# A new address layout for the gate block of a decoder layer, with two raw weight tiles instead of three

## The chip, the cores and the metric

The kernel runs on one NeuronCore of one Trainium2 chip. The metric is the device time of one execution in microseconds (us). A profiled execution also gives the span, from the first to the last recorded instruction, and the granted clock of TensorE as a share of full speed.

The engines are named as in the profile: PE is the matrix engine (PEld its weight loads), DVE the vector engine, ACT the scalar engine, POOL GpSimd. SP issues most of the DMAs. Each engine, and each engine's DMA issues, run strictly in the order in which the program was written out.

## The reference

One layer over 1024 tokens of width 1024, in 32-bit floats. After an RMSNorm giving `h`, three branches (a chunked mLSTM, a differential attention, a cross-attention into memory) are computed, merged by gates, and followed by an MLP:

```python
h = rms_norm(x, norm_mix_g[l])
...
g_m, g_d, g_c = jnp.split(jax.nn.sigmoid(h @ w_gate[l] + b_gate[l]), N_BRANCH, axis=-1)
merged = g_m * (y_m @ w_proj_m[l]) + g_d * (y_d @ w_proj_d[l]) + g_c * (y_c @ w_proj_c[l])
x = x + merged @ w_out[l]
h2 = rms_norm(x, norm_mlp_g[l])
x = x + jnp.square(jax.nn.relu(h2 @ w_up[l])) @ w_down[l]
```

The gates `sigmoid(h @ w_gate + b_gate)` have 3 x 1024 columns. The last 1024 columns (the gate `g_c`) are what the block around this change computes.

## The kernel before

Every float matrix product is made of three matmuls: each operand is split into a rounded part and a remainder, `hi` (a cast on ACT) and `lo` (a subtraction on DVE), and `mm3` adds hi*hi, hi*lo and lo*hi in PSUM. So every weight and every activation passes through one ACT cast and one DVE subtraction before PE reads it (`split`, lines 113 and 114).

The stages follow one another on PE: input norms and memory keys, branch C, branch M, branch D (the attention, with matmuls of the gates and of the next head woven between), then the **gate block** (`wino_gates`, line 1142), then the **tail** (`tail`, line 1405): the three branch projections in the order C, M, D, the output projection, and the MLP.

The gate block uses a Winograd form of the 2 x 2 block product: four units `u`, each with seven products `j` (12 matmuls of 128x512 each) in the order of `PROD`. Its tiles, per SBUF partition:

- `X[4]`, `X[5]`, `X[6]`, `X[3]`: sums of blocks of `h`, 16,384 bytes each, loaded from DRAM (`hc_d`) and split in place. A unit's products 0, 1 and 6 read `hT` itself, product 2 reads X[4], 3 reads X[5], 4 reads X[6] and 5 reads X[3].
- `fr`: raw weights, 8,192 bytes each. Eight of them are loaded (two DMAs each), numbered 2u+kk; POOL adds four derived blocks (lines 1161 to 1164). A ring of three is used. `load(n+3)` is issued when the last of the seven blocks of raw n has been split.
- `w`: the split weights, in a ring of 13 tiles shared with the stages before; 14 are made per unit by `wsp`, and they run ahead of PE by as much as the ring allows.
- `ev`: four evaluation tiles `u2`, `c11`, `u3`, `c21` of 2,048 bytes, with two buffers each. Each product's PSUM bank is added into one of them by DVE (the first by an ACT copy). PE alternates between two PSUM banks, so a product can begin only when the product two before it has been added.
- `gt`: two tiles of 2,048 bytes for the tanh of a finished output, which ACT stores to DRAM (`gates`), on its own DMA queue.

**Addresses set the order of loads.** A pool takes the next free bytes upward. A tile placed on bytes that an earlier, closed pool has used must wait for those users. With `reuse_waits="tile"` (branch D's and the gate block's pools) a tile waits only for the users of earlier tiles on its own bytes. Without it (all the tail's pools) **every** tile of the new pool waits for **every** user of every closed pool that the new pool touches.

`hT` fills 3,072 to 68,608, the ring of 13 `w` tiles 68,608 to 108,544, the ring of raw weights up to 117,760. Above it first lie branch D's pools, and then, over them, the gate block's: in the kernel before `gt` (117,760), `ev` (121,856), X[3] (138,240), X[6] (154,624), X[5] (171,008), X[4] (187,392), `fr` 0 to 2 (203,776 to 228,352).

The tail then lays its own pools over everything: nine single tiles `ys` for a branch's split rows (`kt`, 8,192 bytes each, from 96,768 to 170,496, filled from the top one down), `yrp` with two raw row tiles `kraw` (170,496 to 178,688), `rp2` with two raw weight tiles `raw` (178,688 to 186,880), `wp2` with four split weight tiles `w` (186,880 to 219,648). For each branch `k_tiles` (line 1377) loads eight row tiles of 512 KB through `kraw` and splits them into `kt`; `load_w` (line 132) loads the weights; `group` runs the matmuls, the first group with k outermost, so that PE can start with one `kt` and one `w`.

Only PE's order is pinned by hand in the gate block. The orders of ACT, DVE, POOL and of the DMA issues are set by the framework's planner, which places each instruction by its own estimate of when its inputs are there.

Of the kernel before, what the change touches and what calls it, by code (L numbers as in the profile page):

```python
# [10 lines left out]
F32 = mybir.dt.float32  # L11
# [6 lines left out]
P = 128  # L18
# [13 lines left out]
def f32(ap):  # L32
    return ap.bitcast(F32)
# [40 lines left out]
class Layer:  # L74
# [487 lines left out]
    def m_gates2(self, pool):  # L562
# [5 lines left out]
        self.nc.vector.tensor_copy(self.gcol, ps2[:, 0 : 3 * W])  # L568

    def branch_m(self, pool, gp, tail, gnext):  # L570
        nc, a = self.nc, self.a
        V, G = nc.vector, nc.gpsimd
# [569 lines left out]
    def wino_gates(self, base):  # L1142

        nc, V, A, G = self.nc, self.nc.vector, self.nc.scalar, self.nc.gpsimd
        one = lambda name, bufs=1: base.enter_context(tc.tile_pool(name=name, bufs=bufs, reuse_waits="tile"))
        tc = self.tc
        gtp, ev, x3, x6 = one("fgt", 2), one("fev", 2), one("fx3"), one("fx6")
        x5, x4, r0, r1, r2 = one("fx5"), one("fx4"), one("fr0"), one("fr1"), one("fr2")
        rr = Ring([r2, r1, r0])
        X = {}  # L1150
        for q, p in ((4, x4), (5, x5), (6, x6), (3, x3)):
            X[q] = p.tile([P, 4, 2, 512], F32R, tag="x", name=self.name("hx"))
        raws, W = {}, []

        def load(n):
            if n < 8:
                u, kk = divmod(n, 2)
                r = rr.tile([P, 8, 2, P], F32, tag="fr", name=self.name("fr"))
                for i in range(2):
                    nc.sync.dma_start(r[:, 0:4, i], self.a["wgq"][u][:, 2 * kk + i])  # L1160
                G.tensor_add(r[:, 4], r[:, 0], r[:, 3])
                G.tensor_sub(r[:, 5], r[:, 4], r[:, 1])
                G.tensor_sub(r[:, 6], r[:, 1], r[:, 0])
                G.tensor_sub(r[:, 7], r[:, 2], r[:, 5])
                raws[n] = r

        def wsp():
            n = len(W)
            if n < 56:
                u, r = divmod(n, 14)  # L1170
                j, kk = divmod(r, 2)
                t = self.wp.tile([P, 2, 256], F32R, tag="w", name=self.name("w"))
                self.split(t[:, 0], t[:, 1], raws[2 * u + kk][:, 1 + self.PROD[j][0]].rearrange("p k n -> p (k n)"))
                W.append(t)
                if j == 6:
                    load(2 * u + 3 + kk)

        def x_(q, kp, i):
            if q >= 3:
                return X[q][:, kp, i]  # L1180
            k, hf = divmod(q + 1, 2)
            return self.hT[:, 2 * kp + k, i, hf * 512 : hf * 512 + 512]

        for n in range(3):
            load(n)
        for q in (4, 5, 6, 3):
            k, h = ((0, 1), (1, 0), (0, 0), (1, 1))[q - 3]
            r = f32(X[q][:, :, 1])
            nc.sync.dma_start(r, self.hcd[:, k, :, h * 512 : h * 512 + 512].rearrange("k p n -> p k n"))
            for i in (0, 2):  # L1190
                self.split(X[q][:, i : i + 2, 0], X[q][:, i : i + 2, 1], r[:, i : i + 2])
        for _ in range(9):
            wsp()
        self.pinned = True
        tl = lambda n: ev.tile([P, 512], F32, tag=n, name=self.name(n))
        for u in range(4):
            def out(i, c):
                ft, s = 16 + u * 2 + i // 2, slice(i % 2 * 512, i % 2 * 512 + 512)
                t = gtp.tile([P, 512], F32, tag="gt", name=self.name("gt"))
                A.activation(t, c, AF.Tanh, bias=self.bg[:, ft : ft + 1], scale=0.5)  # L1200
                nc.scalar.dma_start(self.gdr[ft, :, s], t)

            for j, (l, q) in enumerate(self.PROD):
                ps = self.mm_tile()
                for kp in range(4):
                    w = W[u * 14 + 2 * j + kp // 2]
                    c = slice(kp % 2 * P, kp % 2 * P + P)
                    self.mm3(ps, (w[:, 0, c], w[:, 1, c]), (x_(q, kp, 0), x_(q, kp, 1)), kp == 0, kp == 3)
                    if kp % 2:
                        wsp()  # L1210
                if j == 0:
                    u2, c11, u3, c21 = (tl(n) for n in ("u2", "c11", "u3", "c21"))
                    A.copy(u2, ps)
                elif j == 1:
                    V.tensor_add(c11, u2, ps)
                    out(1, c11)
                elif j == 2:
                    V.tensor_add(u2, u2, ps)
                elif j == 3:
                    V.tensor_add(u3, u2, ps)  # L1220
                elif j == 4:
                    V.tensor_add(c21, u3, ps)
                    out(3, c21)
                elif j == 5:
                    V.tensor_add(u3, u3, ps)
                    V.tensor_add(u2, u2, ps)
                    out(2, u3)
                else:
                    V.tensor_add(u2, u2, ps)
                    out(0, u2)  # L1230
        self.pinned = False
# [180 lines left out]
    def tail(self):  # L1412
        tc, nc, a = self.tc, self.nc, self.a
# [10 lines left out]
        with ExitStack() as c0:  # L1424
            E = lambda *x, **k: c0.enter_context(tc.tile_pool(*x, **k))
            one = E(name="tone", bufs=1)
# [7 lines left out]
            with ExitStack() as c1:  # L1434
                E = lambda *x, **k: c1.enter_context(tc.tile_pool(*x, **k))
                self.pmm, self.kmm, self.nmm = Banks(E, "pmm2"), 8, 3
                if True:
# [4 lines left out]
                    hole = E(name="hole", bufs=1).tile([P, 7 * 256], F32, name="hole")  # L1442
                    V.memset(hole[:, 0:1], 0.0)
                    ysp = Ring([E(name=f"ys{i}", bufs=1) for i in range(9)][::-1])
                    rawp = E(name="yrp", bufs=2)
                    self.rp = E(name="rp2", bufs=2)
                    self.wp = E(name="wp2", bufs=4)
                    hi = [[mtp.tile([P, 512], F32R, name=f"mh{k}_{hf}") for hf in range(2)] for k in range(NK)]
# [43 lines left out]
            with ExitStack() as c1:  # L1492
                E = lambda *x, **k: c1.enter_context(tc.tile_pool(*x, **k))
# [237 lines left out]
    def run(self):  # L1731
        tc, nc = self.tc, self.nc
        with ExitStack() as ctx:
            E = lambda *x, **k: ctx.enter_context(tc.tile_pool(*x, **k))
# [22 lines left out]
            with ExitStack() as c1:  # L1757
# [37 lines left out]
                with tc.tile_pool(name="wpg", bufs=13, reuse_waits="tile") as self.wp, tc.tile_pool(name="rpg", bufs=3, reuse_waits="tile") as self.rp:  # L1795
                    self.gwp, self.grp = self.wp, self.rp
                    with ExitStack() as c3:
                        E3 = lambda name, bufs: c3.enter_context(tc.tile_pool(name=name, bufs=bufs, reuse_waits="tile"))
                        pdo, pdy, pd, pd3, pdm = E3("pdo", 2), E3("pdy", 1), E3("pd", 2), E3("pd3", 3), E3("pdm", 1)
                        pdv2, pds, pd5, pdv = E3("pdv2", 17), E3("pds", 1), E3("pd5", 7), E3("pdv", 5)  # L1800
                        self.tmask = pdm.tile([P, D], F32, name="tmask")
                        nc.gpsimd.memset(self.tmask, 0.0)
                        nc.gpsimd.affine_select(
                            out=self.tmask[:, D - P : D], in_=self.tmask[:, D - P : D], pattern=[[-1, P]],
                            compare_op=ALU.is_ge, fill=NEG, base=0, channel_multiplier=1,
                        )
                        self.pd4 = None
                        class T4:
                            def tile(_, shape, dt, tag, name):
                                tag = "dscr2" if tag == "gt" else tag  # L1810
                                p = {
                                    "draw": pd5, "drr": pdv, "dv": pdv2, "dk": self.pd4, "dpe1": pdm, "daT": pd3, "dst": pd3,
                                    "dscr": pds, "dsg": pds, "dscr2": pdy, "y": pdy, "doS": pdo, "dso": pdo,
                                }.get(tag, pd)
                                return p.tile(shape, dt, tag=tag, name=name)
                        self.gpool = T4()
                        kv, done = [], [0]
                        gemm = self.d_gemm(self.gpool, kv, done)
                        next(gemm)
                        sums = self.h_sums(self.gpool)  # L1820
                        for n in range(32):
                            next(self.gates)
                            if n % 2 == 0:
                                next(sums)
                        cg.close()
                        self.pd4 = E3("pd4", 4)
                        self.branch_d(T4(), sums, gemm, kv, done)
                    with ExitStack() as c3:
                        self.wino_gates(c3)
# [70 lines left out]
```

## Time and profile before

| | |
|---|---|
| median of 3 runs | 2200.8 us (2197.91 to 2201.39) |
| the profiled execution's own time | 2198.07 us |
| its span | 2196.3 us, 30710 instructions |
| busy share of the span: PE, DVE, ACT, POOL | 98%, 65%, 46%, 26% |
| mean granted clock of TensorE | 0.996 |
| gate block on PE | from about 1127 to 1206 us |
| first projection group of the tail on PE | from about 1207 us |

A row of the timeline shows the start, the duration, the engine, the line of the kernel, the operation, what it writes and reads, and in brackets how long the engine had been idle and what ended that. Rows of equal instructions are merged (x36 is 36 of them). A row of the windows view gives, for a stretch of time, its length, the busy time and instruction count of PE, PEld, DVE, ACT and POOL, the granted clock, the mean busy share of the DMA engines and what they moved in GB/s.

### The profile page before, as it was taken

The page shows a single profiled execution, that of the slowest core. Times are in us where ns is not written, and L with a number is a line of the kernel's source. Part 1 is how long each engine was busy: PE and PEld are TensorE (multiplying, and loading weights), DVE is VectorE, ACT ScalarE, POOL GpSimd, SP SyncE. Part 2 cuts the span into 40 slices and gives each one's busy share as a digit, 9 for nine tenths or more (in the row PEclk, how much of TensorE's full clock was granted, in tenths as well). Part 3 has the DMA queues.
Part 4 walks back from the last instruction along what each step waited for, and adds up shares of the span by engine and source line. Part 5 has one row for each costly group of instructions (what it writes and reads, how often), then busy time and mean ns, then how long its engine had stood idle before and what let it go on. Part 6 is the DMA issues. An engine that isn't in the chain of part 4 may idle for free.

```text
span 2196.3 us, 30710 instructions
## 1 busy us (share of the span) xinstructions
PE 2154.0 (98%) x11049; PEld 1853.4 (84%) x11049; DVE 1424.0 (65%) x2678; ACT 1002.6 (46%) x1998; POOL 571.6 (26%) x732
## 2 busy tenths in 40 slices
PE   7999999999999999999999999999999999999999
PEld 5878889898899999999887788888787888788887
DVE  6643565575548777777665433554589877867779
ACT  6543354454346666666554221223444444643332
POOL 2100000000111111111121002202757655665553
PEclk9999999999999999999999999999999999999999
DMA  6123122121443343333343643435435444954444
GB/s 245 37 72 116 60 89 70 44 82 49 157 119 92 96 97 86 86 87 80 108 158 121 206 144 125 139 115 190 155 116 199 157 144 153 330 192 157 145 140 168
DMA packets 137358, 281.46 MB, mean 128 GB/s; under 512 B 13137, under 2 KB 29814, under 8 KB 135158
## 3 DMA queue, kind: packets, MB, share of 16 engines
q1 hardware_dynamic: 130870, 259.58, 37.5%
q10 hardware_dynamic: 6336, 19.93, 2.3%
q8 instruction: 87, 1.43, 0.3%
q14 instruction: 65, 0.53, 0.1%
HBM read 182.95 MB, written 71.34 MB: 116 GB/s over the span
## 4 chain that ended last, share of the span: by engine, by line
PE 79%; DMA 7%; DVE 6%; ACT 3%; POOL 2%; issue 2%; SPq 0%; DVEq 0%; ACTq 0%; POOLq 0%
PE mm L93 46%; PE p L93 21%; PE sc L93 6%; PE po L93 3%; PE tp L96 3%; DMA x_d<-gl 1%; DVE acc L69 1%; DVE wo L69 1%; DMA gl<-in_xT 1%; PE pr L96 1%; DMA xr<-h_d 1%; DVE u L69 1%; DMA kraw<-y 1%; POOL wraw L1262 0%; DVE w L114 0%
## 5 line engine op out<-in xcount | busy, mean ns | idle before, releaser
L93 PE MATMUL mm<-w,hT 128*128 128x384 f32 (+3 forms) x2496 | 472.9, 332 | 2.9 <-ACT w L113 2.4
L93 PE MATMUL mm<-hT,w 128*128 128x512 f32 x1680 | 411.8, 396 | 0.0
L93 PEld LDWEIGHTS mm<-w,hT 128*128 128x128 f32 x2496 | 390.2, 190 | 14.5 <-ACT w L113 3.0
L93 PEld LDWEIGHTS mm<-hT,w 128*128 128x128 f32 x1680 | 308.5, 188 | 64.7
L93 PE MATMUL p<-xo,wo 128*128 128x512 f32 x1344 | 309.7, 392 | 3.1 <-DVE u L69 1.6
L93 PE MATMUL p<-xd,wo 128*128 128x512 f32 x1344 | 307.8, 391 | 3.8 <-DVE u L69 1.9
L93 PEld LDWEIGHTS p<-xd,wo 128*128 128x128 f32 x1344 | 252.9, 189 | 58.5 <-DVE u L69 2.6
L93 PEld LDWEIGHTS p<-xo,wo 128*128 128x128 f32 x1344 | 252.2, 189 | 59.3 <-DVE u L69 3.7
L93 PE MATMUL mm<-kt,w 128*128 128x512 f32 x1152 | 264.5, 391 | 4.0 <-ACT kt L113 2.7
L93 PEld LDWEIGHTS mm<-kt,w 128*128 128x128 f32 x1152 | 216.8, 189 | 51.7 <-ACT kt L113 3.8
L113 ACT CAST w<-raw 128x256 fp32r<-128x256 f32 (+3 forms) x272 | 142.2, 545 | 164.7 <-PE mm L93 123.2
L114 DVE TENSOR_TENSOR w<-raw,w 128x256 fp32r<-128x256 f32 (+3 forms) x272 | 162.7, 619 | 80.0 <-ACT w L113 78.6
L106 ACT CAST wo<-wraw 128x896 fp32r<-128x896 f32 x122 | 115.0, 944 | 206.6 <-PE p L93 112.0
L69 DVE TENSOR_TENSOR wo<-wraw,wo 128x896 fp32r<-128x896 f32 x122 | 144.3, 1200 | 57.0 <-ACT wo L106 57.0
L1260 POOL TENSOR_TENSOR wraw<-wraw 128x128 f32<-128x128 f32 x128 | 95.1, 743 | 238.4 <-DMA wraw<-in_wdown 103.5
L1008 ACT ACTIVATE dpe<-sc,dst,drr 128x256 f32<-128x256 f32 (+7 forms) x128 | 106.8, 834 | 97.6 <-DVE dst L1004 95.4
L129 POOL TENSOR_SCALAR hss<-hss 128x4 f32<-128x4 f32 x8 | 3.3, 411 | 416.0 <-ACT mscr L754 273.3
L1000 DVE CUSTOM_DVE_ANT_0 sc<-sc,tmask 128x256 f32<-128x256 f32 (+7 forms) x128 | 97.0, 758 | 13.3 <-PE sc L93 12.6
L1263 POOL TENSOR_TENSOR wraw<-wraw 128x128 f32<-128x128 f32 x128 | 93.9, 733 | 10.0
L93 PE MATMUL sc<-dk,dq 128*128 128x512 f32 (+3 forms) x384 | 92.2, 348 | 0.0
L1262 POOL TENSOR_TENSOR wraw<-wraw 128x128 f32<-128x128 f32 x128 | 91.8, 717 | 0.0
L106 ACT CAST xd<-xd 128x1536 fp32r<-128x1536 f32 (+2 forms) x36 | 54.9, 1528 | 67.7 <-DMA xd<-r_d 67.7
(308 smaller groups left out, 3087.6 us busy)
## 6 DMA issues: line engine op xcount, KB each, us to landing
dk<-dsg SPq DMA_DIRECT2D x64, 256.0 KB, 4.5
wraw<-in_wup SPq DMA_DIRECT2D x64, 256.0 KB, 3.3
r_d<-xts SPq DMA_DIRECT2D x16, 1024.0 KB, 4.1
wraw<-in_wdown SPq DMA_DIRECT2D x64, 256.0 KB, 3.0
xd<-r_d SPq DMA_DIRECT2D x19, 768.0 KB, 7.3
xd<-r_d SPq DMA_DIRECT2D x14, 1024.0 KB, 7.0
raw<-in_wd SPq DMA_DIRECT2D x32, 384.0 KB, 3.2
kraw<-y SPq DMA_DIRECT2D x24, 512.0 KB, 4.5
```

What stands on the lines that cost most here:

```text
L69: return self.tc.keep_in_program_order(f(*a, **k))
L93: self.pin(self.nc.tensor.matmul(out, l, r, start=start, stop=stop))
L96: self.pin(self.nc.tensor.transpose(out, x, self.ident))
L106: self.A.copy(hi, src)
L113: nc.scalar.copy(hi, src)
L114: nc.vector.tensor_sub(lo, src, f32(hi))
L129: g.tensor_scalar(r, ss, 1.0 / width, EPS, op0=ALU.mult, op1=ALU.add)
L1000: V.tensor_tensor_reduce(out=sc[:, 0:n], in0=sc[:, 0:n], in1=self.tmask[:, D - n : D], scale=1.0, scalar=-3.0e38, op0=ALU.add, op1=ALU.max ...
L1008: nc.scalar.activation(pe[c][:, 0:n], sc[:, 0:n], AF.Exp, bias=t8[:, 2 + c : 3 + c], scale=rr[:, i, c : c + 1], accum_out=t8[:, 4 + c : 5 ...
L1260: G.tensor_add(r[:, 4], r[:, 0], r[:, 3])
L1262: G.tensor_sub(r[:, 6], r[:, 1], r[:, 0])
L1263: G.tensor_sub(r[:, 7], r[:, 2], r[:, 5])
```

## The change

Three places change, and all of them are allocations.

1. The gate block's pools are opened in another order. From 117,760 upward: one evaluation pool `ev1` (8,192 bytes), a pad of 128 bytes, X[3], X[6], X[4], `r0`, `r1`, X[5], `gt`, and the second evaluation pool `ev0`. The two evaluation buffers are now two pools, used in turn by units 0, 2 (`ev0`) and 1, 3 (`ev1`). The ring of raw weights has two tiles, used in the order r1, r0; a raw is loaded when the raw two before it has been split. The pad gets one memset.
2. In the tail `yrp` holds three raw row tiles instead of two; `rp2` and `wp2` move up by 4,096 bytes.
3. In branch D the pools `pd` (with `dpe0` and `dq`, two buffers each) and `pd3` (with `daT` and `dst`, three buffers each) change places.

```diff
-        gtp, ev, x3, x6 = one("fgt", 2), one("fev", 2), one("fx3"), one("fx6")
-        x5, x4, r0, r1, r2 = one("fx5"), one("fx4"), one("fr0"), one("fr1"), one("fr2")
-        rr = Ring([r2, r1, r0])
+        ev1, pad, x3, x6, x4, r0, r1, x5, gtp, ev0 = (
+            one(f"f{n}", 2 if n == "gt" else 1)
+            for n in ("ev1", "pd", "x3", "x6", "x4", "r0", "r1", "x5", "gt", "ev0")
+        )
+        nc.vector.memset(pad.tile([P, 32], F32, tag="pad", name="fpd")[:, 0:1], 0.0)
+        rr, ev = Ring([r1, r0]), (ev0, ev1)
...
-                    load(2 * u + 3 + kk)
+                    load(2 * u + 2 + kk)
...
-        for n in range(3):
+        for n in range(2):
             load(n)
...
-        tl = lambda n: ev.tile([P, 512], F32, tag=n, name=self.name(n))
         for u in range(4):
+            tl = lambda n: ev[u % 2].tile([P, 512], F32, tag=n, name=self.name(n))
...
-                    rawp = E(name="yrp", bufs=2)
+                    rawp = E(name="yrp", bufs=3)
...
-                        pdo, pdy, pd, pd3, pdm = E3("pdo", 2), E3("pdy", 1), E3("pd", 2), E3("pd3", 3), E3("pdm", 1)
+                        pdo, pdy, pd3, pd, pdm = E3("pdo", 2), E3("pdy", 1), E3("pd3", 3), E3("pd", 2), E3("pdm", 1)
```

## The prediction

> **What bounds the kernel now.** I read the page's first lines, then the windows view by stage, then PE's timeline where the windows show it idle.
>
> ```profile
> span 2196.3 us, 30710 instructions
> ...
> 600.00:1045.00 445.00, 444.53 (x2845) 430.36 (x2844) 335.80 (x980) 270.21 (x687) 67.56 (x61) 1.00 0.38 96
> 1045.00:1127.00 82.00, 80.52 (x417) 67.76 (x416) 54.27 (x113) 45.50 (x92) 13.76 (x17) 1.00 0.42 136
> 1127.00:1206.00 79.00, 78.34 (x345) 63.99 (x343) 41.03 (x76) 33.80 (x70) 17.14 (x21) 1.00 0.34 115
> 1206.00:1234.00 28.00, 24.27 (x93) 18.23 (x94) 12.80 (x13) 11.36 (x12) 0.04 (x1) 0.94 0.69 241
> 1234.00:1500.00 266.00, 266.00 (x1175) 220.23 (x1174) 110.34 (x125) 55.65 (x63) 28.03 (x28) 1.00 0.41 134
> ```
>
> PE sets the time. The change can win only what PE loses between 1045 and 1234 us: 1.5 us idle at the end of branch D, 0.7 in the gate block, 3.7 at the start of the tail. From 1234 to 1500 PE is never idle, and 266.00 us / 1175 = 0.2264 us per matmul is the pitch I use; a product of 12 takes 2.72 us.
>
> ```profile
> 1108.08 1.01 PE L93 MATMUL po<-dv,daT 128*128 128x128 f32 x7 [1.36 <-DVE daT L114]
> 1156.35 8.48 PE L93 MATMUL mm<-hx,w 128*128 128x512 f32 x36 [0.43 <-DVE c L1215]
> 1202.89 2.88 PE L93 MATMUL mm<-hT,w 128*128 128x512 f32 x12
> 1206.78 1.17 PE L93 MATMUL mm<-kt,w 128*128 128x512 f32 x4 [1.00 <-POOL ones L1428]
> 1208.13 5.52 PE L93 MATMUL mm<-kt,w 128*128 128x512 f32 x21 [0.18 <-DVE kt L114]
> 1215.80 16.42 PE L93 MATMUL mm<-kt,w 128*128 128x512 f32 x63 [2.15 <-ACT kt L113]
> 1232.73 7.59 PE L93 MATMUL mm<-kt,w 128*128 128x512 f32 x32 [0.51 <-ACT kt L113]
> ```
>
> The start of the tail loses more than its idle time. From the end of the gate block (1202.89 + 2.88 = 1205.77) to 1240.32 PE runs 4 + 21 + 63 + 32 = 120 matmuls, 27.2 us at the pitch, in 34.55: **7.4 us lost**, of which 3.84 are the bracketed waits. The rest are slow matmuls:
>
> ```profile
> 1213.00:1218.00 5.00, 2.85 (x11) 2.03 (x10) 3.45 (x3) 2.22 (x3) 0.00 (x0) 0.93 1.03 410
> 1218.00:1223.00 5.00, 5.00 (x17) 3.90 (x17) 0.20 (x1) 0.00 (x0) 0.00 (x0) 0.73 0.68 226
> ```
>
> After the gaps the granted clock falls to 0.93 and 0.73; 5 x 0.07 + 5 x 0.27 = 1.7 us go there. The DMA engines are full (share 1.03).
>
> So all that can be won is 1.36 + 0.43 + 7.4 = 9.2 us, 0.4%.
>
> **The change, part by part.** *Start of the tail.* What does each tail pool wait for?
>
> ```profile
> 1197.65 0.82 SPq L139 DMA_DIRECT2D raw<-in_wpc  x2
> 1200.37 0.80 SPq L1383 DMA_DIRECT2D kraw<-y  x2
> 1201.69 1.05 ACT L113 CAST w<-raw 128x1024 fp32r<-128x1024 f32 x1 [7.96 <-DMA raw<-in_wpc]
> ```
>
> Before, `rp2` (178,688 to 186,880) lies on X[5] alone, and the raws are issued 8.12 us before the gate block's end, three products: exactly when X[5] is done. `yrp` touches X[6] by 512 bytes, and the row loads go out two products before the end, when X[6] is done. `wp2` lies on X[5], X[4] and raws, so its casts wait only for data. The rows come too late: that is the 2.15 and the 0.51.
>
> Afterwards `yrp` (170,496 to 182,784) lies on X[4] and r0. X[4] is last read by product 2, so the row loads can go out at 1205.77 - 4 x 2.72 = 1194.9, 5.5 us earlier, and three at once. The first five `kt` tiles lie on X[4], X[6] and X[3] and are free by 1203. `rp2` (182,784 to 190,976) lies on r0 and r1, free after the last weight split. All this moves away from PE's path. But `wp2` (190,976 to 223,744) now lies on r1, X[5], **`gt`** and `ev0`, and its tiles wait for every user of them, the last store of `gt` to DRAM among them. That store closes the chain of the last product:
>
> ```profile
> 1206.25 0.68 DVE L1229 TENSOR_TENSOR u<-u,mm 128x512 f32<-128x512 f32 x1
> ...
> 1207.62 0.72 ACT L1200 ACTIVATE gt<-u,dv 128x512 f32<-128x512 f32 x1 [0.94 <-DMA gates<-gt]
> ...
> 1208.37 0.33 ACTq L1201 DMA_DIRECT2D gates<-gt  x1
> ...
> L1201 ACTq DMA_DIRECT2D gates<-gt x16: 326/326/387, 1136.7 to 1208.4; - x16
> ...
> DMA to landing us min/median/max: 2.0/2.0/6.5
> ```
>
> PE's first tail matmul then comes after the add (0.68), the tanh up to its store's issue (1208.37 - 1207.62 = 0.75), the landing, and the cast of `w` (1.05). The landing has a median of 2.0 and a maximum of 6.5, the high values while the row loads fill the DMA engines; with those out of the way earlier I take 3.0. The gap is 0.68 + 0.75 + 3.0 + 1.05 = 5.5 us. Queued behind the waiting cast on ACT are only later casts, whose rows are there by then, so PE loses nothing after the gap except the clock, 1.7 as in the rows above. 5.5 + 1.7 = 7.2 lost, against 7.4: **-0.2 us**. Ends: landing 2.0 and no clock loss give 4.5, or -2.9; landing 6.5 gives 9.0 + 1.7, or +3.3.
>
> The Trainium skill speaks against this part (DMA: Bandwidth & Descriptors, Anatomy of one DMA): a transfer's semaphore rises only when the last byte is confirmed in memory, slowest for HBM, with about 2.0 us fixed and the bytes at 436 GB/s on top (fitted there for GpSimd's path; ACT issues this one). Worked out from that page, the 256 KB store would be an estimated 2.6 us and this part -0.6; the trace agrees in part only, with a median of 2.0 below the page's figure and a maximum of 6.5 far above.
>
> *Gate block, ring of two.* A raw's DMAs, its POOL sums and the split that waits:
>
> ```profile
> 1154.32 0.71 ACT L113 CAST w<-fr 128x256 fp32r<-128x256 f32 x2 [2.91 <-DMA fr<-in_wgq]
> ...
> 1154.76 0.94 DVE L114 TENSOR_TENSOR w<-fr,w 128x256 fp32r<-128x256 f32 x1 [2.90 <-ACT w L113]
> 1155.63 0.67 DVE L1215 TENSOR_TENSOR c<-u,mm 128x512 f32<-128x512 f32 x1
> ...
> 1158.85 1.30 DVE L114 TENSOR_TENSOR w<-fr,w 128x256 fp32r<-128x256 f32 x2
> 1160.07 0.68 DVE L1220 TENSOR_TENSOR u<-u,mm 128x512 f32<-128x512 f32 x1
> ...
> 1154.68 0.74 POOL L1161 TENSOR_TENSOR fr<-fr 128x256 f32<-128x256 f32 x1 [13.37 <-DMA fr<-in_wgq]
> ...
> 1159.83 0.92 POOL L1162 TENSOR_TENSOR fr<-fr 128x256 f32<-128x256 f32 x1
> ```
>
> Before, at each unit's change one raw was a unit ahead, and only the other was just in time: its load starts when the split of the last block but one ends, lands 2.91 us too late for ACT, and the add of product 1 behind it on DVE costs PE 0.43. The weights themselves have 13 tiles of lead, so PE never misses a weight; it misses the adds queued behind a late split. Afterwards both raws are just in time. The first lands when the just-in-time one lands now, so the 0.43 stays about what it is. The second raw's sums come behind the first's on POOL, as the second pair here: its block for product 2 (L1162) is ready at 1159.83 + 0.92 = 1160.75 instead of about 1157. The cast (0.41, half of 0.71 and a little), the slow subtraction (0.94) and the add of product 3 (L1220), which stands behind that subtraction on DVE, end at 1162.8. PE wants that bank two products after 1156.35 + 2.72, at 1161.8: **1.0 us** lost per change of unit. There are three. The planner may put an add ahead of a split; I take two thirds, **+2.0**, between -0.4 (all adds ahead) and the second rival's +8.2.
>
> *End of branch D.*
>
> ```profile
> 1067.87 27.32 SPq L1160 DMA_DIRECT2D fr<-in_wgq  x6
> 1096.32 0.37 SPq L1189 DMA_DIRECT2D hx<-hc_d  x1
> 1108.67 2.16 SPq L1189 DMA_DIRECT2D hx<-hc_d  x3
> ...
> 1100.35 4.21 DVE L114 TENSOR_TENSOR w<-fr,w 128x256 fp32r<-128x256 f32 x5
> ...
> 1105.08 2.35 DVE L114 TENSOR_TENSOR hx<-hx 128x1024 fp32r<-128x1024 f32 x2
> 1107.35 0.68 DVE L114 TENSOR_TENSOR daT<-tp,daT 128x512 fp32r<-128x512 f32 x1
> ...
> 1117.36 1.05 ACT L113 CAST hx<-hx 128x1024 fp32r<-128x1024 f32 x1 [1.59 <-DMA hx<-hc_d]
> ```
>
> Before, raws 1 and 2 and X[4] lie on branch D's last keys, and the other X on its values, until 1109. Afterwards X[5] lies on the keys and X[6] on `dpe0` (moved up by the exchange of pools), so both load before 1106, while r0 and X[4] lie on value tiles: raw 1, X[4] and X[3] load last. They are wanted at 1128 or later, so nothing starves. The 1.36 us came from five weight splits at 0.84 each and an X split ahead of `daT` on DVE. One raw fewer means fewer splits and no POOL sums there: **-1.0**, between -1.36 and +1.6 (ACT's longest wait for an X, 1.59, landing on PE).
>
> *The rest.* The pad's memset, the third `kraw` in the later branches and the later start of the block sums of `h` under the exchanged pools cost 0: PE is full from 600 to 1045 and from 1234 to 1500, and the sums are read only from 1096. If that cover went, a memset is the least of it. The MLP's pools meet the same users, the last raw and the last weight of the output projection, 4,096 bytes higher.
>
> Sum: -0.2 + 2.0 - 1.0 = **+0.8 us**, on the profiled 2198.07 (span 2196.3 and 1.8 around it). The median lies 2.7 above the profiled execution, so I forecast 2200.8 + 0.8 = **2201.6 us**.
>
> **Rivals.** *The tail wins.* The last store lands in 2.0 us, the clock holds, and the adds stay ahead in the gate block: -2.9 - 0.4 - 1.4 = -4.7, 2196.1. For it: all rows are in SBUF before PE asks. Against: a gap of 4.5 us where gaps of 2.15 already dropped the clock.
>
> *The ring of two stalls PE (the slower side).* Place: DVE's queue at the three changes of unit. If the add of product 1 stands behind the split of the **second** raw, which lands one weight (half a product, 1.36) later, it ends at 1154.76 + 1.36 + 0.94 + 0.67 = 1157.7 instead of 1155.92, PE's need (1156.35 - 0.43): 1.8 us, and with the 1.0 above, 2.8 to 2.9 per change, 8.6 in all, less today's 0.43: +8.2; with the other parts 2207.8. It decides from the point where the add's end passes 1155.92. For it: today's add already stands behind a late split. Against: the planner sees the second load start later and can reorder.
>
> *The layout moves only what is hidden.* If `wp2`'s wait is met early or replaces an equal one, and the adds keep their slack, nothing moves: 2200.8.
>
> **How the numbers follow.** Forecast 0.53, hidden 0.14, ring stalls 0.18, tail wins 0.15. The forecast's own range is 2198 to 2206. About 0.2% (4.4 us) is what a measurement can tell from no change: below 2196.4 is faster, above 2205.2 slower. Faster: most of the tail's win and a little of the forecast, 0.14; slower: 0.15 of the ring's 0.18 and 0.07 of the forecast, 0.22; the same 0.64. The range 2195 to 2208.5 reaches both rivals.
>
> **What would show it.** The first `w` cast of the tail waits for a store of `gt`, and PE has one gap of 4.5 to 6 us at 1206 instead of four small ones, with no wait for `kt` behind it. Row loads leave near 1195. In the gate block PE waits for the adds of lines 1215 and 1220 near 1136, 1156 and 1175 after POOL's second set of sums. The 1.36 us before `po` shrinks. A first tail matmul before 1208, or PE idle over 4 us between 1127 and 1206, would prove the forecast wrong.

## The result, and the profile after

The changed kernel takes 2205.5 us (median of 18 runs, 2202.1 to 2209.8); 18 runs of the kernel before, taken beside them, have a median of 2199.4. The ratio is **1.0025, 95% interval 1.0018 to 1.0032**: 6.1 us slower, where +0.8 was forecast. The profiled execution took 2206.7 us. The page's first line, then the windows view (length, then busy time and count of PE, PEld, DVE, ACT and POOL, clock, DMA share, GB/s):

```profile
span 2204.9 us, 30710 instructions
```

```profile
600.00:1045.00 445.00, 444.34 (x2843) 430.18 (x2842) 334.66 (x979) 270.84 (x688) 67.92 (x61) 1.00 0.38 95
...
1125.00:1207.00 82.00, 80.62 (x344) 63.55 (x342) 43.95 (x78) 34.41 (x71) 19.86 (x25) 1.00 0.42 136
1206.00:1211.00 5.00, 0.69 (x4) 0.23 (x2) 3.32 (x5) 3.67 (x5) 0.20 (x1) 0.84 0.90 291
1211.00:1216.00 5.00, 0.00 (x0) 0.00 (x0) 1.23 (x1) 1.12 (x2) 0.00 (x0) 0.50 1.00 390
1216.00:1221.00 5.00, 4.67 (x13) 3.34 (x14) 4.75 (x5) 4.01 (x5) 0.00 (x0) 0.64 0.48 158
1221.00:1250.00 29.00, 29.00 (x130) 24.01 (x129) 9.17 (x10) 4.21 (x4) 0.00 (x0) 1.00 0.55 182
```

PE is full up to 1045 and again from 1221, as before. Between 1206 and 1216 it does almost nothing: 0.69 us of work in ten, with the DMA engines at 0.90 and 1.00 and the granted clock at 0.84 and 0.50. Timeline of the changed kernel, PE first, then the chain that ends the gap (its lines lie three higher: L1218 and L1223 are L1215 and L1220 of the kernel before):

```profile
1104.69 2.21 PE L93 MATMUL po<-dv,daT 128*128 128x256 f32 x16 [0.20 <-DVE daT L114]
...
1135.22 9.02 PE L93 MATMUL mm<-hx,w 128*128 128x512 f32 x36 [0.43 <-DVE c L1218]
...
1155.37 9.02 PE L93 MATMUL mm<-hx,w 128*128 128x512 f32 x36 [0.15 <-DVE c L1218]
...
1175.54 9.04 PE L93 MATMUL mm<-hx,w 128*128 128x512 f32 x36 [0.16 <-DVE c L1218]
...
1203.80 2.90 PE L93 MATMUL mm<-hT,w 128*128 128x512 f32 x12
1216.31 46.00 PE L93 MATMUL mm<-kt,w 128*128 128x512 f32 x194 [9.62 <-ACT w L113]
...
1195.59 9.83 SPq L1386 DMA_DIRECT2D kraw<-y  x6
...
1206.66 1.23 DVE L114 TENSOR_TENSOR kt<-kraw,kt 128x1024 fp32r<-128x1024 f32 x1 [0.40 <-ACT kt L113]
1207.81 0.68 DVE L1232 TENSOR_TENSOR u<-u,mm 128x512 f32<-128x512 f32 x1
1207.92 4.98 SPq L1386 DMA_DIRECT2D kraw<-y  x3
1208.18 1.04 ACT L113 CAST kt<-kraw 128x1024 fp32r<-128x1024 f32 x1 [0.93 <-DMA kraw<-y]
1209.13 0.72 ACT L1203 ACTIVATE gt<-u,dv 128x512 f32<-128x512 f32 x1
1209.88 0.33 ACTq L1204 DMA_DIRECT2D gates<-gt  x1
1215.17 1.04 ACT L113 CAST w<-raw 128x1024 fp32r<-128x1024 f32 x1 [3.88 <-DMA gates<-gt]
```

Read from the top:

- The wait for `po` at the end of branch D fell from 1.36 to 0.20: 1.2 us won.
- In the gate block each change of unit shows a short wait for an add, and rows of 36 matmuls that take 9.02 us (8.48 before). The block ran from 1124.88 to 1203.80 + 2.90 = 1206.70, 81.8 us against 78.7: **3.1 lost**. Not all of this is waiting, as the rows below show.
- At the start of the tail the first `w` cast waits for the last store of `gt`, and PE for that cast: one gap of 9.62 us. From 1206.70 to 1216.31 + 46.00 = 1262.31 are 55.6 us; 194 matmuls at the pitch of 0.2264 are 43.9. **11.7 lost**, against 7.4 before: 4.3 more.

The last unit of the gate block has no change of unit behind it and waits for nothing in either kernel. Its 48 matmuls on X, before:

```profile
1192.01 11.04 PE L93 MATMUL mm<-hx,w 128*128 128x512 f32 x48
```

and after:

```profile
1192.61 11.35 PE L93 MATMUL mm<-hx,w 128*128 128x512 f32 x48
```

They take 0.31 us longer. Four units of this are 1.2 of the 3.1, in matmuls that read X at its new places; the other 1.9 is waits and what they slow down.

The three bullets make 6.2 us. The two spans differ by 8.6; the rest is in a place that the prediction held to be full. Groups view of PE between 1540 and 1600 us (the step from the output projection to the MLP; the last figures are idle time and what ended it), before:

```profile
L93 PE MATMUL px<-ones,ssq 128*128 128x1 f32 x16 | 2.1, 251 | 2.2 <-POOL ssq L1483 1.7 <-DVE gl L1476 0.5
```

and after:

```profile
L93 PE MATMUL px<-ones,ssq 128*128 128x1 f32 x16 | 2.9, 302 | 5.0 <-DVE gl L1479 3.3 <-POOL ssq L1486 1.7
```

2.8 us more. Whether the change did this is taken up behind the experiments.

### The profile page after: what moved, and what is told of

Read it like the earlier page. It is cut to its first block, busy times and chain, and to the rows that moved or that the text cites. A ratio compares the mean times of both kernels' runs of the same rounds, so it can differ in the third digit from the quotient of the medians.

```text
span 2204.9 us, 30710 instructions
## 1 busy us (share of the span) xinstructions
PE 2153.2 (98%) x11049; PEld 1851.8 (84%) x11049; DVE 1424.0 (65%) x2679; ACT 1001.6 (45%) x1998; POOL 572.5 (26%) x732
## 3 DMA queue, kind: packets, MB, share of 16 engines
q8 instruction: 87, 1.43, 0.3%
## 4 chain that ended last, share of the span: by engine, by line
PE 82%; DMA 7%; DVE 5%; ACT 2%; POOL 2%; issue 2%; SPq 0%; DVEq 0%; POOLq 0%; ACTq 0%
PE mm L93 47%; PE p L93 22%; PE sc L93 6%; PE po L93 3%; PE tp L96 3%; DVE acc L69 1%; DMA gl<-in_xT 1%; DMA xr<-h_d 1%; DMA fr<-in_wgq 1%; DVE wo L69 1%; PE pr L96 1%; DMA x_d<-gl 1%; DVE u L69 1%; DVE w L114 1%; PE tp L93 0%
## 5 line engine op out<-in xcount | busy, mean ns | idle before, releaser
L1263 POOL TENSOR_TENSOR wraw<-wraw 128x128 f32<-128x128 f32 x128 | 91.5, 715 | 232.2 <-DMA wraw<-in_wdown 101.7
L1266 POOL TENSOR_TENSOR wraw<-wraw 128x128 f32<-128x128 f32 x128 | 91.1, 712 | 9.9
L1265 POOL TENSOR_TENSOR wraw<-wraw 128x128 f32<-128x128 f32 x128 | 92.8, 725 | 0.0
L1264 POOL TENSOR_TENSOR wraw<-wraw 128x128 f32<-128x128 f32 x128 | 87.9, 687 | 0.0
```

## The experiments

My theory after the result: most of the loss is the tail's `w` casts, which wait for a store of `gt` because the tail's pools have no waits by tile; the ring of two costs the gate block some 2 to 3 us; the shorter wait for `po` is a gain. Rivals: the ring alone makes the loss; the third row tile makes it (more row loads in flight); the layout merely shifts the order of the plan. The table holds all runs; the readings of single profiles are made as above: the gate block from PE's rows, the tail's loss from the end of the gate block to about 1262 us against 0.2264 us per matmul.

| kernel | median, us | ratio to before, 95% | gate block | lost at start of tail | wait `po` | waits `px` |
|---|---|---|---|---|---|---|
| before | 2199.4 | | 78.7 | 7.4 | 1.36 | 2.2 |
| after | 2205.5 | 1.0025 (1.0018 to 1.0032) | 81.8 | 11.7 | 0.20 | 5.0 |
| e1: waits by tile for `wp2` | 2203.5 | 1.0018 (1.0005 to 1.0032) | 80.9 | 7.8 | 0.27 | 4.1 |
| e2: `gt` lowest | 2194.9 | 0.9976 (0.9963 to 0.9990) | 80.5 | 0.1 | 0.34 | 0.0 |
| e3: third raw weight | 2205.3 | 1.0019 (1.0005 to 1.0033) | 79.3 | 11.5 | 0.24 | 3.8 |
| e4: e2 and e3 | 2192.4 | 0.9966 (0.9954 to 0.9978) | 79.3 | 0.0 | none | 1.1 |
| e5: before, ring of two | 2202.9 | 1.0018 (1.0003 to 1.0032) | 80.2 | 5.3 | 1.36 | 3.6 |
| e6: before, three row tiles | 2198.3 | 0.9994 (0.9983 to 1.0005) | 78.6 | 3.7 | 1.75 | 1.5 |
| e7: before, `pd` and `pd3` exchanged | 2199.2 | 0.9995 (0.9985 to 1.0005) | 78.2 | 4.7 | 1.69 | 0.6 |
| e8: after, two row tiles | 2206.6 | 1.0032 (1.0021 to 1.0043) | 81.7 | 13.4 | none | 3.2 |
| e9: after, `pd` and `pd3` as before | 2208.5 | 1.0042 (1.0027 to 1.0056) | 81.2 | 12.1 | 0.18 | 4.7 |
| e10: e4, two row tiles | 2195.9 | 0.9988 (0.9975 to 1.0001) | 79.2 | 3.2 | 0.17 | 3.6 |

The ratios are against runs of the kernel before in the same batch (medians 2200.6 for e1 to e4, 2199.8 for e5 to e8, 2198.4 for e9 and e10). e1 to e10 have 12 runs each, e9 six.

### e1: the wait for the store taken away

```diff
-                    self.wp = E(name="wp2", bufs=4)
+                    self.wp = E(name="wp2", bufs=4, reuse_waits="tile")
```

> The changed kernel, except that the split weights of the tail wait only for users of their own bytes; addresses and all orders stay. Theory (the first casts wait for the last store of gt): the cast no longer waits 3.9 us at 1211 to 1215, but it still stands behind the row casts on ACT, so PE starts at about 1212.4 instead of 1216.3; about 4 us of the gap of 9.6 go, and the time falls by 3.5 to 5 us, to about 2201. Rival 1 (the ring of two costs it, the gap only shows what comes late anyway): PE waits for rows instead, less than 1 us is won. Rival 2 (the DMA engines are overfull from earlier rows): the gap stays above 8 us.

Timeline of e1:

```profile
1207.21 0.33 ACTq L1204 DMA_DIRECT2D gates<-gt  x1
...
1208.53 1.04 ACT L113 CAST w<-raw 128x1024 fp32r<-128x1024 f32 x1
...
1209.67 1.19 PE L93 MATMUL mm<-kt,w 128*128 128x512 f32 x2 [4.93 <-issue]
```

The cast no longer waits for the store's landing (it ends at 1209.57, and PE starts 0.1 us later, though the bracket names no releaser), and the gap is 4.93 instead of 9.62 us. The tail's loss falls by 3.9, to 7.8, no lower than before's. Every engine keeps the order of the changed kernel here, so the first `w` cast still stands on ACT behind the `kt` casts and the last tanh, and starts when these are done; its raws had left at 1187.72, 20 us earlier, so it was not short of data. So the wait is one part of the trouble, and the **order** that the planner chose for a cast that it believed late is, by this reading, the other; no run changes the order alone. The median fell by 2.0 us only, less than the 3.5 to 5 expected, and the intervals of the two ratios overlap.

### e2: `gt` opened first

```diff
-        ev1, pad, x3, x6, x4, r0, r1, x5, gtp, ev0 = (
+        gtp, ev1, pad, x3, x6, x4, r0, r1, x5, ev0 = (
```

(with the names in the same order). `gt` then lies at 117,760, under the `kt` tiles, and `wp2` no longer touches it.

> The changed kernel with gt opened first, at 117,760, so that the tail's weights no longer lie on it; all else above moves up by 4,096 bytes. Theory: neither the wait for the store nor the late place in ACT's queue is left, the casts follow the end of X[5] as before the change, and the rows come early; the gap falls from 9.6 to under 1.5 us, the clock holds, and 9 to 10.5 us are won, to about 2196. Rival 1: under 1 us won. Rival 2: rows still late, a gap of 3 to 5 us with waits for kt, 4 us won at most.

Timeline of e2:

```profile
1197.71 2.01 ACT L113 CAST w<-raw 128x1024 fp32r<-128x1024 f32 x2 [4.07 <-PE mm L93]
...
1205.84 56.38 PE L93 MATMUL mm<-kt,w 128*128 128x512 f32 x248
...
1209.32 0.72 ACT L1203 ACTIVATE gt<-u,dv 128x512 f32<-128x512 f32 x1
```

Two `w` casts now run at 1197.71, when X[5] is free (PE's release in the bracket), and PE enters the tail at 1205.84 without a gap, while the last outputs of the gate block are still being finished at 1209. Nothing is lost there. The time is 10.6 us under the changed kernel and below the kernel before. Both the wait and the late order are gone here, so e2 does not separate them. Theory confirmed: the ring of two and the third row tile are still in this kernel, so neither of them makes the gap.

### e3 and e4: the third raw weight put back

```diff
-x5, gtp, ev0 = (
+x5, gtp, ev0, r2 = (
...
-        rr, ev = Ring([r1, r0]), (ev0, ev1)
+        rr, ev = Ring([r2, r1, r0]), (ev0, ev1)
...
-                    load(2 * u + 2 + kk)
+                    load(2 * u + 3 + kk)
...
-        for n in range(2):
+        for n in range(3):
             load(n)
```

e3 is this on the changed kernel, e4 on e2.

> The changed kernel with a third raw weight tile above everything and loads as far ahead as in the kernel before. Theory: the gate block, 81.8 us on PE from its first to its last matmul, falls back to about 78.7; the gap at the tail's start stays at 9 to 10; 2.5 to 3.5 us won, to about 2202.5. Rival 1: all 6 us come back, about 2199.5. Rival (the ring is hidden): nothing.

> Both of the last two: gt first, and a ring of three. Theory: the two gains add, gate block 78.7 us and gap under 1.5 us, 12 to 13 us won on the changed kernel, about 2193, which is 6 us better than the kernel before. If the two gains are one and the same, it ends where the better of the two ends.

Timeline of e3:

```profile
1132.19 11.36 PE L93 MATMUL mm<-hx,w 128*128 128x512 f32 x48
...
1213.77 48.40 PE L93 MATMUL mm<-kt,w 128*128 128x512 f32 x204 [9.27 <-ACT w L113]
```

Timeline of e4:

```profile
1203.24 59.10 PE L93 MATMUL mm<-kt,w 128*128 128x512 f32 x260
```

The waits for adds are gone in e3, and its gate block is 2.6 us shorter; at 79.3 it stays 0.6 above the 78.7 expected, with 48 matmuls on X at 11.36 us, like the changed kernel's 11.35. The gap stays. The median moved by 0.3 us only, where about -3 was expected: a miss in the total, and with intervals of some 3 us each it is not settled how much of the 2.6 reaches the end. In e4 the gate block is 1.1 shorter than in e2 and the median 2.5 lower. **e4 is faster than both kernels**, 0.9966 of before.

### e5: the ring of two alone, in the old layout

```diff
-        rr = Ring([r2, r1, r0])
+        rr = Ring([r1, r0])
...
-                    load(2 * u + 3 + kk)
+                    load(2 * u + 2 + kk)
...
-        for n in range(3):
+        for n in range(2):
```

> Before, with the one edit that the ring of raw weights holds two instead of three; everything else of the change is left out. Theory (each change of unit has the raw tile's next load ahead of its sums, and the rows at the change are stretched): the gate block on PE grows from 78.7 us to 80.5..82, the waits of ACT on fr<-in_wgq and on POOL's sums appear once a change, the start of the tail keeps its two kt waits (2.15 and 0.51), and the time is 2.0 to 3.5 us over before: 2201.4 to 2202.9 if before is 2199.4. Rival (what the gate block loses is given back by waits that it covers later, as the third raw tile put back into the changed kernel moved the median by 0.2 alone): gate block the same 80.5..82, but the time within 1 us of before, 2198.9 to 2200.4.

Timeline of e5:

```profile
1100.49 0.92 POOL L1161 TENSOR_TENSOR fr<-fr 128x256 f32<-128x256 f32 x1
...
1102.05 3.50 DVE L114 TENSOR_TENSOR hx<-hx 128x1024 fp32r<-128x1024 f32 x2 [1.24 <-ACT hx L113]
...
1106.20 2.04 PE L93 MATMUL po<-dv,daT 128*128 128x256 f32 x16 [1.36 <-DVE daT L114]
...
1142.14 3.02 PE L93 MATMUL mm<-hx,w 128*128 128x512 f32 x12 [0.22 <-DVE u L1220]
```

The median is 3.1 us over before (0.7 to 7.0, which does not quite rule out the rival's 1 us), inside the 2.0 to 3.5 expected; the gate block, 80.2, falls just short of the 80.5 to 82 expected, and the two `kt` waits are 1.87 and 0.82 instead of 2.15 and 0.51.

Over the twelve profiles the six with a ring of two have gate blocks of 81.0 on average and the six with three 78.9, 2.2 us less, but five of the six with two also have the new layout. Taken apart, the ring costs **1.7 us** in the old layout (80.2 against 78.5, the mean of before, e6 and e7) and **2.0** in the new (81.2, the mean of the changed kernel, e1, e2, e8 and e9, against 79.3, that of e3, e4 and e10). The layout costs about 0.8 with three raws. The row of the last unit's 48 matmuls on X says the same: 11.35 or 11.36 in all eight profiles with the new layout, 11.04 in all four with the old. The transfers do not explain it: in the first unit e3's row is 11.36 with a DMA share of 0.20, and the kernel before's 11.04 with 0.21. Why the matmuls are slower there is open. X[3] begins at 138,240 in the old layout, a multiple of 1,024, and behind the pad at 126,080 (117,760 + 8,192 + 128) in the new, a multiple of 128 only; no run moves X alone.

It also says something of branch D: with one raw less the wait for `po` is still 1.36.

### e6, e8, e10: the third row tile

```diff
-                    rawp = E(name="yrp", bufs=2)
+                    rawp = E(name="yrp", bufs=3)
```

e6 is this on the kernel before; e8 and e10 undo it in the changed kernel and in e4.

> Before, with a third raw row tile for the branch projections and nothing else of the change. Theory (the second pair of row loads waits at 1208 for a raw tile to come free, and the kt casts of 1214.70 for their landing): the waits of 2.15 and 0.51 us on kt go, and with them some of the low clock behind them; the gate block stays at 78.7; the time is 2.7 to 5 us under before: 2194.4 to 2196.7 if before is 2199.4. Rival (the row loads are late because the engines of the transfers are full at the end of the gate block, not for want of a tile): the waits stay within 1 us of 2.7 in sum, and the time within 1 us of before.

> The changed kernel with two raw row tiles for the branch projections instead of three; the rest of the change stays. Theory (the last store of gt lands 5.2 us after its issue because six row loads left ahead of it at 1195.59): with four loads ahead it lands in 2.5 to 4 us, the gap at the start of the tail falls from 9.6 to 7..8.5 us; a kt wait of up to 2 us comes back behind it; in sum 1 us less to 1 us more than after: 2204.5 to 2206.5. Rival 1 (the landing is late for another reason): gap 9.3 to 10 and kt waits on top, 2206 to 2209. Rival 2 (the third row tile, not the wait on the store, is what loses the time at the start of the tail): the gap falls under 4 us and the time to 2200 or less.

> The version with gt lowest and a third raw weight tile, with two raw row tiles for the branch projections instead of three. Theory (once no cast waits for a store, the third raw row tile is what keeps the rows ahead of PE at the start of the tail): waits of 1 to 3 us on kt come back near 1205 to 1215 and the time is 1 to 3.5 us over the version with three, 2193.4 to 2196 if before is 2199.6. Rival (the row loads leave early enough with two as well, since the tiles they split into are free by then): no wait on kt over 0.5 us and the time within 1 us of 2192.

Timeline of e6:

```profile
1210.35 2.11 PE L93 MATMUL mm<-kt,w 128*128 128x512 f32 x8 [0.57 <-DVE kt L114]
1212.91 0.51 PE L93 MATMUL mm<-kt,w 128*128 128x512 f32 x1 [0.46 <-ACT kt L113]
1214.17 48.12 PE L93 MATMUL mm<-kt,w 128*128 128x512 f32 x211 [0.75 <-DVE kt L114]
```

Timeline of e8:

```profile
1215.29 47.08 PE L93 MATMUL mm<-kt,w 128*128 128x512 f32 x193 [10.02 <-ACT w L113]
```

and the line view of its stores of `gt` (e8, line 1204):

```profile
DMA to landing us min/median/max: 2.0/2.0/5.2
```

Timeline of e10:

```profile
1217.53 5.55 PE L93 MATMUL mm<-kt,w 128*128 128x512 f32 x23 [0.76 <-DVE kt L114]
1223.63 0.49 PE L93 MATMUL mm<-kt,w 128*128 128x512 f32 x1 [0.55 <-ACT kt L113]
1224.89 37.47 PE L93 MATMUL mm<-kt,w 128*128 128x512 f32 x164 [0.76 <-DVE kt L114]
```

In e6 the wait of 2.15 for `kt` is gone and the loss is 3.7; the median fell by 1.4 us, inside its uncertainty and short of the 2.7 to 5 expected. The profile alone does not show that the third tile did it: e7, with two row tiles, has `kt` waits of 0.73 and 0.64 and loses 4.7. In e10 waits of 0.76, 0.55 and 0.76 come back and the median is 3.5 us over e4: theory confirmed, though each wait is below the 1 to 3 us that I named. In e8 the gap is 10.02 and the last store lands in 5.2 us as in the changed kernel, with four row loads in the first round instead of six: rival 1, without the `kt` waits that it had on top. So the third row tile did **not** cost the time and did not make the store late. It is a gain in e4 against e10, 3.2 us in the tail's loss and 3.5 between the medians (ratios of 0.9966 and 0.9988, from two batches). In the changed kernel less of it shows: 1.7 in the profile (13.4 against 11.7) and 1.1 between the medians, with overlapping intervals.

### e7 and e9: the exchange of `pd` and `pd3`

```diff
-                        pdo, pdy, pd, pd3, pdm = E3("pdo", 2), E3("pdy", 1), E3("pd", 2), E3("pd3", 3), E3("pdm", 1)
+                        pdo, pdy, pd3, pd, pdm = E3("pdo", 2), E3("pdy", 1), E3("pd3", 3), E3("pd", 2), E3("pdm", 1)
```

e7 is this on the kernel before, e9 undoes it in the changed kernel.

> Before, with the pools pd and pd3 exchanged and nothing else of the change: every engine keeps the order of its instructions, only addresses of the tiles at the end of branch D move. Theory (the shorter wait for po, 1.36 to 0.20, comes from this exchange): the wait on po is under 0.4 and the time 0.5 to 1.3 us under before, 2198.1 to 2198.9 if before is 2199.4. Rival (the wait for po differs from one execution or layout to the next for another reason): it stays over 1.0 and the time is within 0.5 us of before.

> The changed kernel with the pools pd and pd3 back in their old places; the rest of the change stays. Theory (the wait for po at the end of branch D became short because the planner, with one raw less to split ahead, puts fewer subtractions of weights ahead of daT on DVE, and the exchange has no part in it): the wait on po stays under 0.4 us and the time within 1 us of the changed kernel, 2204.5 to 2206.5 if before is 2199.6. Rival (in the new layout it is the exchange that lets the X load early): the wait on po is 1.0 to 1.8 us and the time 1 to 2 us over the changed kernel, 2206.5 to 2207.5. For the waits of PE on px at the step to the MLP (2.2 us in before's profile, 5.0 in the changed kernel's): if they belong to the change they are 4 to 6 us here, if they differ from one execution to the next they may be anything from 0 to 5.

Timeline of e7:

```profile
1108.10 1.01 PE L93 MATMUL po<-dv,daT 128*128 128x128 f32 x7 [1.69 <-DVE daT L114]
```

Timeline of e9:

```profile
1106.00 2.24 PE L93 MATMUL po<-dv,daT 128*128 128x256 f32 x16 [0.18 <-DVE daT L114]
```

The exchange has no part in the shorter wait. Nor has the ring: e5 has two raws and keeps the wait, e3, e4 and e10 have three in the new layout and wait 0.24 at most. What is left, by elimination, is the **places** of the gate block's tiles. How they do it is less clear. In e5, as in before, POOL forms its sums of raws (rows of line 1161 and on) while DVE subtracts for X, and two subtractions take 3.50 us. The same view of the changed kernel:

```profile
1101.30 1.23 DVE L114 TENSOR_TENSOR hx<-hx 128x1024 fp32r<-128x1024 f32 x1 [2.71 <-ACT hx L113]
1102.82 1.23 DVE L114 TENSOR_TENSOR hx<-hx 128x1024 fp32r<-128x1024 f32 x1 [0.29 <-ACT hx L113]
1103.96 0.68 DVE L114 TENSOR_TENSOR daT<-tp,daT 128x512 fp32r<-128x512 f32 x1
1105.15 0.69 DVE L114 TENSOR_TENSOR daT<-tp,daT 128x512 fp32r<-128x512 f32 x1 [0.51 <-ACT daT L113]
...
1109.17 0.19 POOL L129 TENSOR_SCALAR dso<-dso 128x4 f32<-128x4 f32 x1 [33.09 <-DVE dso L1071]
```

POOL had been idle for 33 us, each subtraction for X takes 1.23, DVE idles ahead of them instead of splitting weights, and both of `daT` follow by 1105.15, where before the second came at 1107.35. That the sums slow DVE is read from these rows; no run was made for it alone. And POOL's sums are not what makes the wait. In e4 they fall in the same place, DVE's subtractions are slow too, and PE does not wait for `po` at all. Timeline of e4, DVE and POOL:

```profile
1098.35 2.91 DVE L114 TENSOR_TENSOR hx<-hx 128x1024 fp32r<-128x1024 f32 x2 [0.59 <-ACT hx L113]
...
1102.95 0.68 DVE L114 TENSOR_TENSOR daT<-tp,daT 128x512 fp32r<-128x512 f32 x1
...
1100.13 1.73 POOL L1166 TENSOR_TENSOR fr<-fr 128x256 f32<-128x256 f32 x1
```

What e4 shares with the changed kernel is that the subtractions for X stand ahead of the first `daT`; in before they stand between the two. But in e5 they stand ahead of it as well, later, and the wait is there. So the places of the tiles bring the work on X forward, which fits all these rows; no run shows it by itself. e9's total, 2208.5 from six runs, is above the expected 2204.5 to 2206.5; its interval overlaps that of the changed kernel, so a cost of undoing the exchange stays open.

### The step to the MLP

Is the 2.8 us there the change's? In the twelve profiles the waits for `px` go from 0.0 to 5.0 us. e8 has the changed kernel's order on PE and shows 3.2, not 5.0; e7 has before's order on every engine and shows 0.6, not 2.2. They go with how far the profiled execution lies from its kernel's median: the five that lie above it (after, e1, e3, e9, e10, by 0.2 to 1.4 us) show 3.6 to 5.0; of the seven that lie below it (by 1.3 to 5.9 us) five (before, e2, e4, e6, e7) show 0.0 to 2.2, and e5 and e8 3.6 and 3.2. So most of this difference seems to belong to the single executions. Without it the profiles differ by 5.8 us, the medians by 6.1. That it is wholly unconnected with the layout is not shown.

## Why the prediction was right or wrong

**The time.** 2205.5 us lies inside the range of 2195 to 2208.5, but that is luck more than foresight: the range was made wide enough to reach both rivals. The sum behind the forecast was +0.8, and the measured difference is +6.1 (4.0 to 7.0), which by the prediction's own limit of 2205.2 is the outcome "slower", to which it gave 0.22. The forecast also counted from a median of 3 runs, 2200.8; from the 2199.4 of 18 runs it would have been 2200.2, and 2205.5 would lie above the forecast's own range too.

**What bounds the kernel** was right but for one thing: I took before's 7.4 us lost at the start of the tail as fixed. e7, with the same order on every engine, lost 4.7. One execution is not precise to 3 us there, and the +4.3 below has that uncertainty.

**Start of the tail, forecast -0.2, measured +4.3.** This step failed. The mechanism was right as far as it went: the first cast waits for the last store of `gt`, one gap, row loads at 1195.59, no `kt` wait behind it. Its terms were too small:

| term | forecast | measured |
|---|---|---|
| product's end to the add's end | 0.68 | 1.79 (1207.81 + 0.68 - 1206.70) |
| to the store's issue | 0.75 | 1.39 (1209.88 - 1208.49) |
| landing | 3.0 | 5.2 |
| cast | 1.05 | 1.04 |
| lost with the clock | 1.7 | 2.1 (11.7 - 9.62) |

I gave the add and the tanh no queue. The rows shown in the prediction already had 2.60 us from the end of the last product (1205.77) to the store's issue (1208.37), of which I took the add and the tanh alone, 1.43; in the changed kernel it is 3.18. The earlier rows had to be split somewhere: they were split in just these microseconds, and a `kt` subtraction of 1.23 us stands ahead of the add, a `kt` cast of 1.04 ahead of the tanh. And I let the row loads be "out of the way": three more leave SP from 1207.92, the DMA engines are at 1.00 (390 GB/s), and the store lands in 5.2 us, between my 3.0 and my upper bound of 6.5. In none of the twelve kernels does the slowest store of `gt` land in less than 4.9 us. The sum of 11.7 passes even the bound worked out there (9.0 + 1.7). I had also expected only later casts behind the waiting `w` cast on ACT; instead the planner put `kt` casts and the last tanh ahead of it. e1 shows that with this order and without the wait 7.8 us are still lost, and e2 that without either 0.1 is.

**Gate block, forecast +2.0, measured +3.1 in this pair.** The ring's part of it, 1.7 to 2.0 by the experiments, is right in size, and DVE's queue is the right place: after POOL's second set of sums, the adds come late. ACT's wait for that second set is in the row of 1139.40 below; the add of line 1223 stands behind its split, as the step has it, and ends at 1141.13. The share of each add is not as forecast: the waits in brackets (0.43, 0.15 and 0.16) are for the add of product 1, which I had left as it was, and PE's next product after the add of line 1223 begins at 1141.19, a wait too short for a bracket, where I had 1.0. The other 1.2 us, the slower matmuls on X, I had put at nothing: I took one pitch for all places.

```profile
1138.45 0.92 POOL L1165 TENSOR_TENSOR fr<-fr 128x256 f32<-128x256 f32 x1
1139.40 1.02 ACT L113 CAST w<-fr 128x256 fp32r<-128x256 f32 x3 [2.06 <-POOL fr L1165]
...
1139.84 0.69 DVE L114 TENSOR_TENSOR w<-fr,w 128x256 fp32r<-128x256 f32 x1 [0.19 <-ACT w L113]
1140.46 0.67 DVE L1223 TENSOR_TENSOR u<-u,mm 128x512 f32<-128x512 f32 x1
```

**End of branch D, forecast -1.0, measured -1.2.** The size was right, the cause half: I put it down to one raw fewer. e5 has one raw fewer and keeps the 1.36. e4 has POOL's sums there and does not wait, so the "no POOL sums there" of the prediction was not the reason either. What remains is the new places of the tiles; how they shorten the wait stays open.

**The rest, forecast 0.** The exchange of pools is 0 in the old layout (e7, -0.6 with an interval of -3.3 to +1.1). The third row tile is not 0 but a gain where the gap is away (e4 against e10).

**The rivals.** "The tail wins" had the right prize, the wrong kernel: it is what e2 and e4 do. "The ring stalls PE", the slower side, came near in its time (2207.8) by another mechanism than its own: the ring cost 1.7 to 2.0, not 8.2. The loss that made the kernel slower arose in the part that I had put at -0.2, and went beyond the +3.3 that I had set as its bound.

## What to carry to other kernels

When a pool without waits by tile is laid over a closed one, look for the latest user that it touches, above all a store to DRAM: its landing becomes part of the wait, and the planner orders the new tile's work as late as it believes that wait. Put the tiles with the latest users under something that is needed late. And cost a chain at a change of stage with the queues of the stage that comes: work that has been made earlier has to run somewhere, and here it ran ahead of the chain that everything waited for.

## What was not expected of the hardware

- A 256 KB store that lands in 2.0 us at the median took 5.2 when row loads of 512 KB went out around it with the DMA engines full (e3 5.4, e8 5.2, e1 5.6). The slowest store of `gt` took 4.9 to 6.6 us in all twelve kernels. The Trainium skill (DMA: Bandwidth & Descriptors, Queues, rings and completion order) states that the semaphore's write lands only after every earlier write of that DMA engine, across its queues. The 5.2 agrees with it, but no run here separates this from a plain sharing of bandwidth.
- In the gap of 9.62 us the granted clock fell to 0.50 in the window from 1211, and was 0.64 in the next, where PE worked again. The Trainium skill (TensorE: Matmul & The Clock Gate, HAM oscillation) warns of idle gaps over about 3.4 us; this trace agrees for the long gap, but the window with 0.73 in the kernel before followed waits of at most 2.15 us, shorter than the page's figure.
- Two DVE subtractions of 128x1024 took 1.23 us each with POOL idle (the changed kernel) and 3.50 (e5) or 2.91 (e4) together beside POOL's sums.
- 48 matmuls on X took 11.04 us in the four kernels with the old layout and 11.35 or 11.36 in the eight with the new one, at a granted clock of 1.00 in both. The cause is open.
